# A chunked mixer trunk on one core: bank hand-overs in the planner of the order, and small copies and sums moved to ScalarE

## The chip, the core and the metric

The kernel runs on one core of a Trainium2 chip. Times are device microseconds (us) of one execution. Five engines work side by side, each through a queue of its own in order: TensorE (PE in the profile; PEld are its weight loads), VectorE (DVE), ScalarE (ACT), GpSimd (POOL) and the queue of SyncE (SP), which issues the transfers. The time before is the median of 3 runs, 2519.05 us (2516.93 to 2519.32).

## The reference

Two layers over 2048 rows of width 1024, in float32. Each layer normalises x and modulates it by a vector from c, projects it once, and gives the pieces to two groups of four heads: gated linear attention in chunks of 64 rows, and differential softmax attention. What the change touches is in the second group:

```python
q = rms_norm(q.reshape(B, S, DIFF_HEADS, 2, DIFF_DH), qn_g) * (DIFF_DH ** -0.5)
k = rms_norm(k.reshape(B, S, DIFF_HEADS, 2, DIFF_DH), kn_g)
s = einsum('bqhmd,bkhmd->bhmqk', q, k)           # two maps m a head
s = where(key_chunk <= q_chunk, s, -inf)
p = softmax(s)
o = einsum('bhqk,bkhe->bqhe', p[:, :, 0] - lam * p[:, :, 1], v)
o = rms_norm(o, g_out) * (1.0 - lam_init) * silu(z)
```

and in the first one the low-rank gate, `log_sigmoid((glr @ w_gk + b_gk)) / 16`. Both groups' outputs are projected by `w_out`, scaled by a gate and added to x.

## The kernel before

The rows are worked in units of 512 (four units a layer, `NU`), a unit in four blocks of 128 rows (`TT`). A float32 product is made of float32r ones: a matrix is split into a rounded part and the rest (`hi`, `lo`, `qh`, `ql`, `hhi`, `hlo`, `oh`, `ol`), and three of the four partial products are summed in PSUM (`mm3`). In a profile these are the acc matmuls of 128x512.

PSUM has eight banks of 512 columns. Four are the ring `acc` of the projections; the other four are one ring of tag `tp`, from which the scores (`sc`), the transposes (`tp`) and the attention outputs (`po`) are all taken.

For each unit and each of the four attention heads, `head_proj` makes a projection of 512 columns (q, k, v, z) into four acc banks. `head_evac` (line 978) takes them out: q and k to `rw`, v to `Vt`, the gate z by a tanh. `qk_gen` (line 1002) transposes q (g = 0) and k (g = 1) into one tp bank each, and forms from them the two operands of the scores. The queries need 128 partitions of which the upper and lower half hold the same: for each map m, ScalarE writes the rounded part `qh` in its own half, VectorE the rest `ql`, and both are written into the other half too (lines 1017 to 1021). `Kt` holds the rounded key in its own half and the rest in the other (lines 1023, 1024), so that one matmul with `qh` and one with `ql` give the whole score.

`attn_gen` (line 1032) takes the keys and values of earlier units back from DRAM (`Kj`, `Vj`), makes the scores of one block and map into s (128 x up to 2048), subtracting the running minimum of the negated score on VectorE, and the exponential on ScalarE with its sums `ls`. Line 1074 to 1082 form the factor `r` and the difference of both maps in `at`. `pv` (line 1085) transposes `at` in fours of 128 columns, copies them to `aT` on ScalarE, and multiplies by the values into `po`; from the sum of squares of `po` (`oss`), GpSimd makes the factor `wq`, and VectorE writes the block into `z`. `gla_gen` (line 818) makes the gate of the other group: lines 835 to 837 write the low-rank gate's rounded part, a second copy of it and its rest into `gT`, all three from the PSUM tile `gps`.

The order in which the engines get their instructions is not that of the code. `Program.record` (line 144) notes every operation with its inputs. `order` (line 244) then plays the program through with a time for each operation and each way from one engine to another, gives a tile a place in its ring when its turn comes, and always takes the operation that can start first; `best_order` (line 211) repeats that 60 times with operations moved ahead that kept TensorE waiting, and keeps the best. The instructions are issued in that order (`issue`, line 348), which is why nearly every row of the profile has line 355. When they are issued, the tile framework adds the waits. Among these is one that `order` does not know: two engines that touch one PSUM tile, reading too, take turns in the order of issue.

Of the kernel before, what the change touches and what calls it, by code (L numbers as in the profile page):

```python
# [12 lines left out]
F32 = mybir.dt.float32  # L13
# [3 lines left out]
AF = mybir.ActivationFunctionType  # L17
ALU = mybir.AluOpType
# [4 lines left out]
P = 128  # L23
# [5 lines left out]
EPS = 1e-6  # L29
# [91 lines left out]
class Program:  # L121
# [6 lines left out]

    def __init__(self, **engines):
        self.ops = []  # L130
        self.hist = {}
        self.group = {}
        self.engines = engines
# [10 lines left out]
    def record(self, e, method, args, kw):  # L144
        i = len(self.ops)
        views = [v for v in list(args) + list(kw.values()) if isinstance(v, View)]
        out = kw["out"] if "out" in kw else args[0]
        deps = set()
        for v in views:
            wr = v is out or v is kw.get("accum_out")  # L150
            h = self.hist.setdefault(v.buf, [])
            keep = []
            for j, w2, box in h:
                hit = all(a < d and c < b for (a, b), (c, d) in zip(box, v.box))
                if hit and (wr or w2) and j != i:
                    deps.add(j)
                if not (wr and all(c <= a and b <= d for (a, b), (c, d) in zip(box, v.box))):
                    keep.append((j, w2, box))
            keep.append((i, wr, v.box))
            self.hist[v.buf] = keep  # L160
        self.ops.append((e, method, args, kw, deps, self.cost(e, method, args, kw, out), {v.buf: 0 for v in views}))

    def together(self, first):

# [46 lines left out]
    def best_order(self, rounds=60):  # L211


        ops, rnd = self.ops, random.Random(0)
        turn = [float(i) for i in range(len(ops))]
        made = self.order(turn)
        best = self.span
        for _ in range(rounds):
            res, begin, end, ready = made
            lines = {e: [i for i in res if ops[i][0] == e] for e in "TAV"}  # L220
            place = {i: k for q in lines.values() for k, i in enumerate(q)}
            waits = [(begin[i] - end[j], i) for j, i in zip(lines["T"], lines["T"][1:]) if begin[i] - end[j] > 150]
            turn2 = list(turn)
            for wait, i in waits:
                if rnd.random() >= wait / 1500 * rnd.random():
                    continue
                first = begin[i] - 15000
                for _ in range(12):
                    e = ops[i][0]
                    i = max(ops[i][4], key=lambda j: end[j] + self.LAT[ops[j][0]][e], default=None)  # L230
                    if i is None or end[i] < first:
                        break
                    if (ops[i][0] in "AV" or ops[i][0] == "T" and i not in self.group) and begin[i] - ready[i] > 80:
                        q, k = lines[ops[i][0]], place[i] - 1
                        while k >= 0 and begin[q[k]] >= ready[i]:
                            turn2[i] = min(turn2[i], turn[q[k]] - 0.5)
                            k -= 1
            made2 = self.order(turn2)
            if self.span <= best:
                best, made, turn = self.span, made2, turn2  # L240
        self.span = best
        return made[0]

    def order(self, turn_of):
        ops, N = self.ops, len(self.ops)
        begin, finish = [0.0] * N, [0.0] * N
        left, uses, turn = {}, [], {}
        for o in ops:
            for b in o[6]:
# [2 lines left out]
                    turn.setdefault((b.pool, b.tag), []).append(b)  # L252
                left[b] += 1
        place = {b: k for q in turn.values() for k, b in enumerate(q)}
        nxt = dict.fromkeys(turn, 0)
        slots = {t: [{} for _ in range(q[0].bufs or q[0].pool.bufs)] for t, q in turn.items()}
        blocked = {t: [] for t in turn}
        slot, used = {}, {}
# [14 lines left out]
        while len(res) < N:  # L273
            while todo:
                now, todo = sorted(todo), []
                for i in now:
                    e, bufs = ops[i][0], ops[i][6]
                    new = {}
                    for b in sorted((b for b in bufs if b not in slot), key=place.get):
                        t = (b.pool, b.tag)  # L280
                        if place[b] != nxt[t] + new.get(t, 0) or len(slots[t]) <= new.get(t, 0):
                            blocked[t].append(i)
                            break
                        new[t] = new.get(t, 0) + 1
                    else:
                        for b in sorted(bufs, key=place.get):
                            if b not in slot:
                                t = (b.pool, b.tag)
                                slot[b] = min(slots[t], key=lambda u: max(u.values(), default=0.0))
                                slots[t].remove(slot[b])  # L290
                                used[b] = {}
                                nxt[t] += 1
                                todo += blocked[t]
                                blocked[t] = []
                            for e2, x in slot[b].items():
                                ready[i] = max(ready[i], x + (self.LAT[e2][e] if e != e2 or e == "S" else 0))
                        heapq.heappush(pend[e], (ready[i], turn_of[i], i))
# [5 lines left out]
            if rest:  # L303
                i = min(rest)[1]
                avail[e].remove(min(rest))
                heapq.heapify(avail[e])
            else:
                i = heapq.heappop(avail[e])[1]
            if e == "T":
                burst = self.group.get(i, 0)  # L310
            if e == "S":
# [31 lines left out]
                    todo += blocked[t_]  # L343
                    blocked[t_] = []
        self.span = max(free.values()) / 1e3
        return res, begin, finish, ready

    def issue(self):
        real = lambda v: v.real() if isinstance(v, View) else v
# [9 lines left out]
def trunk_kernel(ctx, tc, x, c, w_ada, b_ada, norm_g, w_in, conv_w, w_gk, b_gk, gla_norm_g,  # L359
# [458 lines left out]
    def gla_gen(l, u):  # L818
# [14 lines left out]
        gT = p_q.tile([98, 512], F32R, tag="uT", name="gT", bufs=2)  # L833
        A.activation(gT[96:98, :], ones[96:98, 0:1].to_broadcast([2, 512]), AF.Copy, scale=-1.0)
        V.tensor_copy(gT[0:32, :], gps[0:32, :])
        A.copy(gT[64:96, :], gps[0:32, :])
        V.tensor_tensor(gT[32:64, :], gps[0:32, :], gT[0:32, :].bitcast(F32), op=ALU.subtract)
        yield pe(3.5, 1.5)
        la = p_q.tile([P, TT, 256], F32, tag="q", name="la")
# [138 lines left out]
    def head_evac(l, u, hd, banks):  # L978
        key = l * NU + u
        ss = p_sm.tile([P, TT, 4], F32, tag="qss", name="qss", bufs=2)  # L980
        rq = p_sm.tile([P, TT, 4], F32, tag="rq", name="rq", bufs=2)
        sz = p_z.tile([P, TT, P], F32, tag="z", name="z")
        Vt = p_kv.tile([P, TT, P], F32, tag="V", name="Vt")
        qk = []
        for t in range(TT):
            rw = p_t.tile([P, 256], F32, tag="rw", name="rw", bufs=4)
            A.copy(rw, banks[t][:, 0:256])
            th = p_t.tile([P, P], F32, tag="th", name="th", bufs=2)
            A.activation(th, banks[t][:, 384:512], AF.Tanh, scale=0.5)
            V.scalar_tensor_tensor(sz[:, t, :], th, 1.0, banks[t][:, 384:512], op0=ALU.add, op1=ALU.mult)  # L990
            A.copy(Vt[:, t, :], banks[t][:, 256:384])
            sq = p_t.tile([P, 256], F32, tag="sq", name="sq", bufs=2)
            A.activation(sq, rw, AF.Square)
            V.tensor_reduce(ss[:, t, :], sq.rearrange("p (a n) -> p a n", a=4), axis=AX.X, op=ALU.add)
            qk.append(rw)
        rsqrt(rq.rearrange("p t a -> p (t a)"), ss.rearrange("p t a -> p (t a)"), 1.0 / 64, EPS)
        for t in range(TT):
            rv = qk[t].rearrange("p (a n) -> p a n", a=4)
            V.tensor_tensor(rv, rv, rq[:, t, :].unsqueeze(2).to_broadcast([P, 4, 64]), op=ALU.mult)
        HD[key, hd] = (qk, Vt, sz)  # L1000

    def qk_gen(l, u, hd):
# [7 lines left out]
        for g in range(2):  # L1010
# [3 lines left out]
            for m in range(2):  # L1014
                own, other = slice(64 * m, 64 * m + 64), slice(64 - 64 * m, 128 - 64 * m)
                if g == 0:
                    A.activation(qh[own, m, :], ps[own, :], AF.Copy, scale=y.G[own, :])
                    V.scalar_tensor_tensor(ql[own, m, :], ps[own, :], y.G[own, :], qh[own, m, :].bitcast(F32),
                                           op0=ALU.mult, op1=ALU.subtract)
                    A.activation(qh[other, m, :], ps[own, :], AF.Copy, scale=y.G[own, :])  # L1020
                    V.tensor_copy(ql[other, m, :], ql[own, m, :].bitcast(F32))
                else:
                    A.copy(Kt[own, m, :], ps[own, :])
                    V.tensor_tensor(Kt[other, m, :], ps[own, :], Kt[own, m, :].bitcast(F32), op=ALU.subtract)
# [7 lines left out]
    def attn_gen(l, u, hd):  # L1032
# [16 lines left out]
        def scores(qt, m):  # L1049
# [23 lines left out]
            if m == 1:  # L1073
                r = p_sm.tile([P, 2], F32, tag="r", name="r")
                V.reciprocal(r[:, 0:1], ls[:, 1:2])
                V.scalar_tensor_tensor(r[:, 0:1], r[:, 0:1], y.nlam, ls[:, 0:1], op0=ALU.mult, op1=ALU.mult)
                V.scalar_tensor_tensor(r[:, 1:2], ls[:, 0:1], EPS, ls[:, 0:1], op0=ALU.mult, op1=ALU.mult)
                at, b = q_s.pop((qt, 0)), q_s.pop((qt, 1))
                for c0 in range(0, nk, 512):
                    c1 = min(nk, c0 + 512)  # L1080
# [4 lines left out]
        def pv(qt):  # L1085
# [30 lines left out]
            junk = p_t.tile([P, P], F32, tag="th", name="junk", bufs=2)  # L1116
            ss = p_sm.tile([P, 2], F32, tag="oss", name="oss")
            A.activation(junk, o_, AF.Square, accum_out=ss[:, 0:1])
            V.scalar_tensor_tensor(ss[:, 1:2], ss[:, 0:1], 1.0 / P, r[:, 1:2], op0=ALU.mult, op1=ALU.add)
            wq = p_sm.tile([P, 1], F32, tag="wq", name="wq")  # L1120
            G.tensor_tensor(wq, ss[:, 1:2], mhalf[:, 0:1], op=ALU.pow)
            V.scalar_tensor_tensor(sz[:, qt, :], o_, wq, sz[:, qt, :], op0=ALU.mult, op1=ALU.mult)
# [205 lines left out]
```

## Time and profile before

| | |
|---|---|
| median of 3 runs | 2519.05 us |
| time of the profiled execution | 2520.62 us |
| its span, first to last instruction | 2518.9 us |
| PE busy | 2465.0 us, 98% |
| DVE busy | 1736.4 us, 69% |
| ACT busy | 1285.0 us, 51% |
| POOL busy | 136.2 us, 5% |

Shares are of the span. Busy is the time in which an engine had at least one instruction running; matmuls overlap, and their ends are modelled. 1.7 us of the execution lie outside the span.

### The profile page before, as it was taken

The numbers are of one execution on the slowest core, as the hardware profiler recorded it, in microseconds if no ns is written. First come the engines' busy times: TensorE is split into PE (matmuls) and PEld (weight loads), VectorE is DVE, ScalarE is ACT, GpSimd is POOL, SyncE is SP. The second block draws the span as 40 slices with busy tenths as digits, with TensorE's granted clock in tenths as the row PEclk, the third lists the DMA queues.
The fourth block names the chain that finished last, engine by engine and source line by source line (L and its number), as shares of the span: only waits on it lengthen the run. The fifth ranks groups of instructions, "written<-read, shape, count | busy, mean of one in ns | idle before, by whom it ended". The sixth has DMA issues, their size and how long they took to land.

```text
span 2518.9 us, 40492 instructions
## 1 busy us (share of the span) xinstructions
PE 2465.0 (98%) x13923; PEld 2025.2 (80%) x13923; DVE 1736.4 (69%) x5313; ACT 1285.0 (51%) x2760; POOL 136.2 (5%) x424
## 2 busy tenths in 40 slices
PE   8999999999999999999999999999999999999999
PEld 5787777887888888888688777888788888888887
DVE  4879767772777737677874884667636777286874
ACT  5656534562445534455763563445614556154552
POOL 0001000000000000000000010000000000000000
PEclk9999999999999999999999999999999999999999
DMA  8667876456453555444357767454474443734343
GB/s 266 251 233 281 286 247 208 156 191 211 163 186 105 189 186 172 141 136 163 109 204 267 265 247 254 169 187 153 161 251 153 142 162 119 262 102 147 130 147 126
DMA packets 204685, 474.00 MB, mean 188 GB/s; under 512 B 20736, under 2 KB 82368, under 8 KB 204480
## 3 DMA queue, kind: packets, MB, share of 16 engines
q1 hardware_dynamic: 204480, 471.41, 54.5%
q8 instruction: 111, 1.82, 0.3%
q14 instruction: 94, 0.77, 0.1%
HBM read 360.19 MB, written 111.15 MB: 187 GB/s over the span
## 4 chain that ended last, share of the span: by engine, by line
PE 79%; DVE 11%; ACT 5%; DMA 3%; issue 2%; POOL 0%; SPq 0%; POOLq 0%; ACTq 0%; DVEq 0%
PE acc L355 51%; PE sc L355 12%; PE po L355 9%; PE tp L355 7%; DVE s L355 3%; ACT qh L355 2%; DVE t L355 1%; DVE ql L355 1%; ACT s L355 1%; DMA wr<-in_w_ada_dram 1%; DVE w L355 1%; ACT t L355 1%; DVE am L355 1%; DMA Kj<-kd 1%; DVE r L355 0%
## 5 line engine op out<-in xcount | busy, mean ns | idle before, releaser
L355 PE MATMUL acc<-w,hhi 128*128 128x512 f32 x2560 | 840.5, 402 | 2.9 <-ACT w L355 1.4
L355 PEld LDWEIGHTS acc<-w,hhi 128*128 128x128 f32 x2560 | 463.7, 189 | 92.3 <-issue 4.8
L355 PE MATMUL acc<-w,hlo 128*128 128x512 f32 x1280 | 504.9, 394 | 0.0
L355 ACT ACTIVATE s<-s,mx 128x512 f32<-128x512 f32 (+15 forms) x256 | 308.2, 1204 | 291.4 <-DVE s L355 290.1
L355 PE MATMUL acc<-hhi,w 128*128 128x512 f32 x1024 | 360.0, 400 | 0.0
L355 PE MATMUL acc<-w,oh 128*128 128x512 f32 x1024 | 332.5, 398 | 2.7 <-DVE t L355 1.1
L355 DVE TENSOR_SCALAR_CACHE_REDUCE s<-sc,mx 64x64 f32<-64x64 f32 (+5 forms) x640 | 307.9, 485 | 33.0 <-PE sc L355 14.3
L355 PEld LDWEIGHTS acc<-w,hlo 128*128 128x128 f32 x1280 | 240.8, 188 | 49.0 <-issue 0.6
L355 PEld LDWEIGHTS acc<-w,oh 128*128 128x128 f32 x1024 | 189.6, 188 | 41.3 <-DVE t L355 2.6
L355 PEld LDWEIGHTS acc<-hhi,w 128*128 128x128 f32 x1024 | 192.0, 188 | 36.7 <-DVE w L355 0.4
L355 ACT COPY aT<-tp 128x512 f32<-128x512 f32 (+2 forms) x320 | 163.0, 523 | 88.2 <-PE tp L355 85.4
L355 PE MATMUL po<-Vj,aT 128*128 128x128 f32 x1536 | 204.4, 277 | 0.7 <-ACT aT L355 0.5
L355 PE MATMUL acc<-w,ol 128*128 128x512 f32 x512 | 201.5, 397 | 0.0
L355 PE MATMUL acc<-hlo,w 128*128 128x512 f32 x512 | 201.0, 393 | 0.0
L355 DVE SCALAR_TENSOR_TENSOR s<-s,r 128x512 f32<-128x512 f32 (+3 forms) x320 | 197.8, 667 | 3.0
L355 PEld LDWEIGHTS po<-Vj,aT 128*128 128x128 f32 x1536 | 190.4, 192 | 10.5 <-ACT aT L355 4.7
L355 DVE TENSOR_SCALAR_CACHE_REDUCE s<-sc 128x512 f32<-128x512 f32 (+4 forms) x256 | 158.2, 621 | 38.7 <-PE sc L355 34.5
L355 PE MATMUL tp<-ident,s 128*128 128x128 f32 x1088 | 172.9, 275 | 11.8 <-DVE ql L355 4.2
L355 PEld LDWEIGHTS tp<-ident,s 128*128 128x128 f32 x1088 | 131.9, 141 | 49.5 <-issue 12.8
L355 ACT COPY rw<-acc 128x256 f32<-128x256 f32 x128 | 48.1, 376 | 239.6 <-PE acc L355 239.6
L355 PE MATMUL sc<-Kj,qh 128*128 128x512 f32 x384 | 158.5, 413 | 3.3 <-DVE s L355 1.4
L355 ACT ACTIVATE qh<-tp,G 64x512 fp32r<-64x512 f32 x128 | 87.6, 684 | 137.1 <-PE tp L355 115.0
(183 smaller groups left out, 3682.8 us busy)
## 6 DMA issues: line engine op xcount, KB each, us to landing
w<-wd SPq DMA_DIRECT2D x424, 512.0 KB, 4.2
wd<-w SPq DMA_DIRECT2D x144, 512.0 KB, 3.7
raw<-in_w_in_dram SPq DMA_DIRECT2D x120, 256.0 KB, 5.0
Kj<-kd SPq DMA_DIRECT2D x48, 512.0 KB, 5.8
wr<-in_w_ada_dram SPq DMA_DIRECT2D x128, 128.0 KB, 3.2
kd<-Kt SPq DMA_DIRECT2D x24, 512.0 KB, 4.0
Vj<-vd SPq DMA_DIRECT2D x48, 256.0 KB, 5.4
wr<-in_w_ada_dram SPq DMA_DIRECT2D x8, 1024.0 KB, 7.4
```

The lines of the kernel that those rows point to most:

```text
L355: getattr(self.engines[e], method)(*[real(a) for a in args], **{k: real(v) for k, v in kw.items()})
```

## The change

Two things change in the planner. `order` now holds PSUM tiles apart: an operation on a PSUM tile is not begun before the last one of another engine on the same tile is over and has reached it (`bank`, `hold`), and `best_order` follows such holds back like inputs. And a ring may be passed: the second tile in line may take a place before the first, if two places are free.

Five operations change in the kernel. The second copies of `qh` and of the gate's rounded part are taken from the first copy in SBUF and not from PSUM again. The second copy of `ql` goes from VectorE to ScalarE. The copy of v stands ahead of the tanh. The square of the sum `ls` (part of `r`), and the sum that gives `oss` its second column, go from VectorE to ScalarE.

```diff
@@ order @@
-                        if place[b] != nxt[t] + new.get(t, 0) or len(slots[t]) <= new.get(t, 0):
+                        ahead = left_out[t].index(b, 0, 2) if b in left_out[t][:2] else N
+                        if len(slots[t]) <= ahead or new.get(t, 0) and ahead != new[t]:
...
+            prior = [j for b in self.banks[i] for e2, j in bank.setdefault(b, {}).items() if e2 != e]
+            if prior:
+                last = max(prior, key=lambda j: finish[j] + self.LAT[ops[j][0]][e])
+                hold = finish[last] + self.LAT[ops[last][0]][e]
+                if hold > t:
+                    held[i], ready[i] = last, hold
+                    if not rest:
+                        heapq.heappush(pend[e], (hold, turn_of[i], i))
+                        continue
+                    t = hold
+            for b in self.banks[i]:
+                bank[b][e] = i
@@ gla_gen @@
-        A.copy(gT[64:96, :], gps[0:32, :])
+        A.copy(gT[64:96, :], gT[0:32, :].bitcast(F32))
@@ head_evac @@
             A.copy(rw, banks[t][:, 0:256])
+            A.copy(Vt[:, t, :], banks[t][:, 256:384])
             th = p_t.tile([P, P], F32, tag="th", name="th", bufs=2)
             A.activation(th, banks[t][:, 384:512], AF.Tanh, scale=0.5)
             V.scalar_tensor_tensor(sz[:, t, :], th, 1.0, banks[t][:, 384:512], op0=ALU.add, op1=ALU.mult)
-            A.copy(Vt[:, t, :], banks[t][:, 256:384])
@@ qk_gen @@
-                    A.activation(qh[other, m, :], ps[own, :], AF.Copy, scale=y.G[own, :])
-                    V.tensor_copy(ql[other, m, :], ql[own, m, :].bitcast(F32))
+                    A.copy(qh[other, m, :], qh[own, m, :].bitcast(F32))
+                    A.copy(ql[other, m, :], ql[own, m, :].bitcast(F32))
@@ attn_gen, scores @@
-                V.scalar_tensor_tensor(r[:, 1:2], ls[:, 0:1], EPS, ls[:, 0:1], op0=ALU.mult, op1=ALU.mult)
+                A.activation(r[:, 1:2], ls[:, 0:1], AF.Square, scale=math.sqrt(EPS))
@@ attn_gen, pv @@
-            V.scalar_tensor_tensor(ss[:, 1:2], ss[:, 0:1], 1.0 / P, r[:, 1:2], op0=ALU.mult, op1=ALU.add)
+            A.activation(ss[:, 1:2], ss[:, 0:1], AF.Identity, scale=1.0 / P, bias=r[:, 1:2])
```

The new planner puts nearly the whole program in another order. Two places show how. The first is ScalarE's queue at the second head of the first unit, before (`qh`, `ql` and `Kt` are the score operands, `oh` a transposed output block, `w` weights, `s` scores, `oss` the sum of squares):

```order
L355 CAST w<-raw 128x512 x2
L355 ACTIVATE junk,oss<-po 128x128
L355 ACTIVATE qh<-tp,G_614 64x512 x4
L355 ACTIVATE oh<-tp,dg_619 128x512
L355 CAST Kt<-tp 64x512 x2
L355 CAST w<-raw 128x512 x4
```

and the same place after:

```order
L370 ACTIVATE oss<-oss,r 128x1
L370 CAST w<-raw 128x512 x2
L370 ACTIVATE qh<-tp,G_636 64x512 x2
L370 CAST qh<-qh 64x512 x2
L370 CAST ql<-ql 64x512 x2
L370 ACTIVATE oh<-tp,dg_643 128x512
L370 CAST Kt<-tp 64x512 x2
L370 CAST w<-raw 128x512 x2
```

Two of the four `qh` operations no longer read the tp tile, and the two `ql` copies have come into this queue, ahead of the `Kt` operations.

The second place is TensorE's queue for the same head, from the transposes of k (the second `tp<-ident,rw`) to the first score with the new key; before:

```order
L355 MATMUL tp<-ident,rw 128x128 x4
L355 MATMUL acc<-hhi,w 128x512
L355 MATMUL acc<-hlo,w 128x512
L355 MATMUL acc<-hhi,w 128x512 x2
L355 MATMUL acc<-hlo,w 128x512
L355 MATMUL acc<-hhi,w 128x512 x2
L355 MATMUL acc<-hlo,w 128x512
L355 MATMUL acc<-hhi,w 128x512 x2
L355 MATMUL acc<-hlo,w 128x512
L355 MATMUL acc<-hhi,w 128x512 x2
L355 MATMUL acc<-hlo,w 128x512
L355 MATMUL sc<-Kt,qh 128x128
```

and after, the last rows of the same stretch (in front of them stand the four transposes of k and eight more acc matmuls):

```order
L370 MATMUL acc<-hhi,w 128x512 x2
L370 MATMUL acc<-hlo,w 128x512
L370 MATMUL acc<-hhi,w 128x512 x2
L370 MATMUL acc<-hlo,w 128x512
L370 MATMUL acc<-hhi,w 128x512 x2
L370 MATMUL acc<-hlo,w 128x512
L370 MATMUL acc<-hhi,w 128x512 x2
L370 MATMUL acc<-hlo,w 128x512
L370 MATMUL acc<-hhi,w 128x512 x2
L370 MATMUL acc<-hlo,w 128x512
L370 MATMUL sc<-Kt,qh 128x128
```

Between the transposes of k and the first score stand 14 acc matmuls before and 23 after. From the transposes of q on it is 20 acc matmuls and eight transposes before, and 27 acc matmuls and eight transposes after.

## Rows read from the trace of the kernel before

**Rows 1.** The page: busy time, share of the span, instructions.
```profile
PE 2465.0 (98%) x13923; PEld 2025.2 (80%) x13923; DVE 1736.4 (69%) x5313; ACT 1285.0 (51%) x2760; POOL 136.2 (5%) x424
```

**Rows 2.** What TensorE's matmuls waited for: us in total, times, longest.
```profile
PE sc L355 <- DVE Kt L355: 7.4, 11, 1.1
...
PE tp L355 <- DVE ql L355: 4.2, 4, 1.1
PE tp L355 <- DVE s L355: 4.0, 7, 1.5
PE tp L355 <- DVE z L355: 3.1, 6, 1.5
...
PE sc L355 <- DVE s L355: 2.4, 6, 0.6
...
PE tp L355 <- ACT aT L355: 1.8, 2, 0.9
...
PE sc L355 <- DVE gT L355: 0.4, 1, 0.4
```

**Rows 3.** Timeline, second head: start, length in us; idle before, releaser in brackets.
```profile
103.14 1.38 ACT L355 ACTIVATE qh<-tp,G 64x512 fp32r<-64x512 f32 x2 [3.50 <-PE tp L355]
...
104.56 0.74 DVE L355 SCALAR_TENSOR_TENSOR ql<-tp,G,qh 64x512 fp32r<-64x512 f32 x1 [1.94 <-ACT qh L355]
...
105.33 1.38 ACT L355 ACTIVATE qh<-tp,G 64x512 fp32r<-64x512 f32 x2 [0.81 <-DVE ql L355]
105.44 0.39 PE L355 MATMUL acc<-hlo,w 128*128 128x512 f32 x1
...
105.67 0.62 PE L355 MATMUL acc<-hhi,w 128*128 128x512 f32 x2
...
107.33 1.16 ACT L355 CAST Kt<-tp 64x512 fp32r<-64x512 f32 x2
...
108.78 1.41 DVE L355 TENSOR_TENSOR Kt<-tp,Kt 64x512 fp32r<-64x512 f32 x2
...
109.51 0.33 PE L355 MATMUL sc<-Kt,qh 128*128 128x128 f32 x1 [0.94 <-DVE Kt L355]
```

**Rows 4.** Timeline at 826 us, a later head of layer 0.
```profile
826.36 1.38 ACT L355 ACTIVATE qh<-tp,G 64x512 fp32r<-64x512 f32 x2 [0.59 <-PE tp L355]
...
829.96 0.76 DVE L355 SCALAR_TENSOR_TENSOR ql<-tp,G,qh 64x512 fp32r<-64x512 f32 x1 [0.99 <-ACT qh L355]
...
830.86 0.63 PE L355 MATMUL tp<-ident,s 128*128 128x128 f32 x4 [1.05 <-DVE ql L355]
```

**Rows 5.** Timeline at 1032 us, a later head of layer 0.
```profile
1031.99 1.38 ACT L355 ACTIVATE qh<-tp,G 64x512 fp32r<-64x512 f32 x2 [0.81 <-DVE ql L355]
...
1033.40 0.59 ACT L355 COPY aT<-tp 128x512 f32<-128x512 f32 x1
...
1034.04 0.66 PE L355 MATMUL tp<-ident,s 128*128 128x128 f32 x4 [0.88 <-ACT aT L355]
```

**Rows 6.** Groups by form: operation, count, busy us, mean ns, idle before it.
```profile
L355 ACT CAST w<-raw 128x512 fp32r<-128x512 f32 x152 | 92.1, 625 | 88.1 <-PE acc L355 69.5 <-DMA wd<-w 9.6 <-DMA raw<-in_w_in_dram 4.2
...
L355 ACT ACTIVATE qh<-tp,G 64x512 fp32r<-64x512 f32 x128 | 87.6, 684 | 137.1 <-PE tp L355 115.0 <-DVE ql L355 21.2
...
L355 ACT ACTIVATE junk<-po 128x128 f32<-128x128 f32 x128 | 35.8, 280 | 121.6 <-PE po L355 120.9
...
L355 ACT ACTIVATE l<-l 128x2 f32<-128x2 f32 x2 | 0.4, 203 | 1.3 <-DVE l L355 1.3
...
L355 DVE SCALAR_TENSOR_TENSOR ql<-tp,G,qh 64x512 fp32r<-64x512 f32 x64 | 48.0, 749 | 84.0 <-ACT qh L355 80.3 <-PE po L355 3.3
...
L355 DVE CAST ql<-ql 64x512 fp32r<-64x512 f32 x64 | 27.0, 422 | 2.0
...
L355 DVE SCALAR_TENSOR_TENSOR r<-ls 128x1 f32<-128x1 f32 x128 | 19.9, 156 | 7.6 <-ACT s L355 6.2
L355 DVE SCALAR_TENSOR_TENSOR oss<-oss,r 128x1 f32<-128x1 f32 x128 | 19.7, 154 | 48.6 <-ACT junk L355 48.4
```

More of the change, by code (lines that the diff above doesn't have):

```diff
@@ L130, in __init__ @@
         self.ops = []
+        self.banks = []
         self.hist = {}
@@ L161, in record @@
         self.ops.append((e, method, args, kw, deps, self.cost(e, method, args, kw, out), {v.buf: 0 for v in views}))
+        self.banks.append({v.buf: 0 for v in views if v.buf.psum})
     def together(self, first):
@@ L218, in best_order @@
         for _ in range(rounds):
-            res, begin, end, ready = made
+            res, begin, end, ready, held = made
             lines = {e: [i for i in res if ops[i][0] == e] for e in "TAV"}
@@ L229, in best_order @@
                     e = ops[i][0]
-                    i = max(ops[i][4], key=lambda j: end[j] + self.LAT[ops[j][0]][e], default=None)
+                    i = max(ops[i][4] | {held.get(i, i)} - {i}, key=lambda j: end[j] + self.LAT[ops[j][0]][e], default=None)
                     if i is None or end[i] < first:
@@ L245, in order @@
         ops, N = self.ops, len(self.ops)
-        begin, finish = [0.0] * N, [0.0] * N
+        begin, finish, held, bank = [0.0] * N, [0.0] * N, {}, {}
         left, uses, turn = {}, [], {}
@@ L254, in order @@
         place = {b: k for q in turn.values() for k, b in enumerate(q)}
-        nxt = dict.fromkeys(turn, 0)
+        left_out = {t: list(q) for t, q in turn.items()}
         slots = {t: [{} for _ in range(q[0].bufs or q[0].pool.bufs)] for t, q in turn.items()}
@@ L291, in order @@
                                 used[b] = {}
-                                nxt[t] += 1
+                                left_out[t].remove(b)
                                 todo += blocked[t]
@@ L345, in order @@
         self.span = max(free.values()) / 1e3
-        return res, begin, finish, ready
+        return res, begin, finish, ready, held
     def issue(self):
```

## The prediction

> **What bounds the kernel now.** First the page: TensorE is busy for 98% of the span, every other engine well below [rows 1]. So the time is TensorE's own work and the places where it waits, and I read the waits next, for TensorE's matmuls alone [rows 2]. The reader is to see how small they are. The largest inside the program is that of the first score with a new key for VectorE's part of it (`Kt`), 7.4 us at 11 places; the next, 4.2 us at 4 places, is a transpose that wants a PSUM tile which `ql` is still reading. The matmuls themselves are the same before and after, so nothing but these waits, and others like them, can be gained or lost: all that the rows name comes to a few tens of us, about 1% of the time.
>
> Then I went to the places on the timeline. At the second head the transposes of q are done and ScalarE starts the first two `qh` at 103.14 [rows 3]. Both read the q tile. VectorE's `ql`, which reads it too, starts at 104.56, when both are over. The next two `qh` start at 105.33, when `ql` is over, having idled 0.81 us with the releaser `ql`, though they need nothing from it: it is the turn on the tile that they wait for. Only behind the fourth `qh` come the `Kt` operations at 107.33, and VectorE's `Kt` at 108.78. TensorE had run out of what stood ahead of the first score and sat idle for 0.94 us up to 109.51. The same ping-pong ends otherwise at 826 us [rows 4]: the tile is held from 826.36 to 829.96 + 0.76 = 830.72, that is 4.36 us, and a transpose that takes its place in the ring idles 1.05 us, until 830.86. At 1032 us [rows 5] it is an `aT` copy that stands on ScalarE behind the second pair of `qh`, and a transpose loses 0.88 us. The planner of before counted on none of this, as it let ScalarE and VectorE read a tile at one time; the order that it wrote has too little TensorE work in front of these three kinds of place.
>
> An idle microsecond in these rows is a little more in lost time. A matmul of 512 columns is shown 0.39 us long, but the next starts 0.23 us after it (105.44 to 105.67) [rows 3]; the 0.16 us of overlap are lost too when the next one waits. Lost time is thus the idle time plus 0.16 us a wait.
>
> **The change part by part.** *The key.* In the new order ScalarE does at this head: two `qh` from the tile (2 x 0.684), two copies of them in SBUF, two copies of `ql`, one `oh`, two `Kt` (1.16). No row shows ScalarE copying 64x512 from SBUF; the nearest are the 128x512 cast from SBUF, 0.625, and from above the 64x512 from PSUM with a factor, 0.684 [rows 6]; below, half of the 1.16 of the two `Kt`, 0.58 [rows 3]. I take 0.625, the same source and the same rounding. The first `Kt` part of VectorE is then ready 1.37 + 1.25 + 1.25 + 0.69 (`oh`, priced as `qh`) + 1.16 + 0.70 (half of 1.41) = 6.4 us after the first `qh`, against 108.78 + 0.70 - 103.14 = 6.3 us before. So the chain to the key is not shorter. What changes is TensorE's side. Before, it came to the first score at 109.51 - 0.94 - 0.16 = 108.41, that is 5.3 us after the first `qh`, with 20 matmuls of 512 columns and 8 transposes since the transposes of q. Now 27 and 8 stand there: 7 x 0.23 = 1.6 us more, 6.9 us, which covers the 6.4 with 0.5 to spare. At all 32 heads, counted with 0.23 us for a matmul of 512 columns and a transpose as half of one, this stretch was shorter than 5.5 us 12 times; after, 4 times, and in those four the order puts the first `Kt` ahead of at least one of the two `ql` copies, which takes 0.6 us or more out of the chain. So I let all 11 waits go: 7.4 + 11 x 0.16 = 9.2 us. If the four copies cost 0.684 each, the chain is 0.24 us longer and still covered.
>
> *The tile of q.* It is read by two `qh` and then two `ql`: 2 x 0.684 + 2 x 0.749 = 2.9 us, where it was held 4.36 us. The 1.46 us saved are more than the 1.05 us that the transpose waited, and the order leaves as much in front of that transpose as before (ten matmuls of 512 columns, where nine stood, beside the same others). 4.2 + 4 x 0.16 = 4.8 us go. What is late next there is the transpose's own data, s, which this trace shows ready.
>
> *aT behind the ping-pong.* ScalarE no longer waits 0.81 us for `ql` between two pairs of `qh` [rows 5], so the copy comes that much sooner, nearly all of the 0.88 us: 2 x (0.81 + 0.16) = 1.9 us, if the new copies stand behind it.
>
> *The gate's copy.* The copy to `gT` from SBUF takes ScalarE's turn out of the tile; TensorE waited for it 0.4 us once [rows 2], and that goes.
>
> *v ahead of the tanh.* VectorE's z stood behind all three of ScalarE's reads of the bank before, and does now: nothing, unless z stood between tanh and v before.
>
> *Work moved.* VectorE loses the 64 `ql` copies (27.0 us), the 128 squares (19.9) and the 128 sums (19.7) [rows 6]: 66.6 us, and comes to 1670. ScalarE gains 64 x 0.625 = 40, loses 64 x 0.059 = 4 on the `qh` copies, and gains 256 operations on one column. Nearest for those is the exponential of two columns, 0.203; above it 128 columns with a sum, 0.280 [rows 6]. With 0.203 it is 52 us, in all +88, and 1373 us, 55% of the span; with 0.280 +108. None of it lies on TensorE's path by itself; ScalarE's share of the span leaves room, and the sum `oss` now follows its squares on the engine that made them. From this I take nothing. For the range I keep 6 us lost (a dozen new waits of 0.35 + 0.16 us behind ScalarE's new operations) and 6 us gained (half of the waits for VectorE's s and z, 4.0 + 3.1 + 2.4 us at 19 places, with their overlap [rows 2]).
>
> A rule of the Trainium skill speaks against this part. "ScalarE: Activation LUTs", section "Rules for kernel authors", gives copies, sums and products to VectorE and keeps ScalarE for functions. By this trace the rule prices it rightly: 66.6 us of VectorE become 88 to 108 us of ScalarE; engine time that nobody waits for is not in the sum, though. Were it to count, it would do so by way of ScalarE's queue: the slower rival below.
>
> The sum: 9.2 + 4.8 + 1.9 + 0.4 = 16.3 us less. The profiled execution took 2520.6 us (span 2518.9 and 1.7 around it), so it would be 2504.3; the median of the three runs lies 1.6 below that execution, which gives 2519.05 - 16.3 = 2502.7.
>
> **Rivals.** *ScalarE becomes late (slower).* Four copies now stand on ScalarE between the last `qh` and `Kt` at most heads, and what comes behind them waits 2.5 us. The point from which it decides is the 0.5 us to spare at the head above. If a copy takes 0.9 us and not 0.625 (nothing in the rows shows one from SBUF to the other half of the partitions), the four are 1.1 us longer and the key 0.6 late; at 20 heads that is 20 x (0.6 + 0.16) = 15 us where 9.2 were lost before. An `aT` copy behind them would cost TensorE the same 0.6 + 0.16 at some ten heads, 7.6 us, and the 1.9 us of the term on `aT` would not come. With 4.8 + 0.4 still saved: 15 - 9.2 + 7.6 - 5.2 = 8 us more, 2527. For it: the chain is no shorter than before, and the rule just named prices such copies as a loss. Against: all forms of 512 columns on ScalarE in [rows 6] lie between 0.58 and 0.69 us, whatever they read.
>
> *The waits move (no change).* The search for the order starts anew, and the places it cured may come back elsewhere: transposes for s, z for the output, the boundary between the layers. If 13 of the 16.3 us come back as new waits, the time is 2515.8. For it: the rest of the waits in [rows 2] are of kinds that the change does not touch, and the order is new everywhere. Against: the new planner sees the turns on the tiles, so what it leaves is less by surprise.
>
> *VectorE was the tighter engine (much faster).* 66.6 us off VectorE also take the waits for s and z away, 9.5 us and 19 x 0.16 = 3 us. Then it is 2502.7 - 12.5 = 2490. For it: VectorE is at 69%, the busiest after TensorE. Against: at such places ScalarE is in the same chain.
>
> **How the numbers follow.** Forecast (2494 to 2511): 0.70. VectorE's relief: 0.12. Waits move: 0.11. ScalarE late: 0.07. The likeliest case gives 2502.7. The range 2489 to 2516 leaves out the slower case, and part of the two others. About 0.2%, 5 us, is what can be told from no change here; faster than 2514 is the forecast, the relief and a small part of the third: 0.84; within: 0.09; slower: 0.07.
>
> **What would show it.** In the waits of TensorE: `Kt` under 1.5 us (now 7.4), `ql` under 1 us (now 4.2), both as idle time. On ScalarE's timeline no wait between the first two `qh` and the rest, and the q tile held about 3 us. VectorE near 1670 us, ScalarE 1360 to 1400. TensorE's matmul work unchanged. I am wrong if the time falls without these two waits going, or if they go and the time stays: then others have come, and the waits name them; wrong in the step on ScalarE if `aT` or `Kt` of ScalarE rise in that list above 5 us.

## The result, and the profile after

The changed kernel takes 2493.85 us (median of 4 runs, 2492.93 to 2495.07) against 2519.19 us (4 runs, 2516.93 to 2520.24) for the kernel before on the same chip: a ratio of 0.9894, with a 95% interval of 0.9880 to 0.9908. The medians differ by 25.3 us (their own ratio would be 0.9899). The forecast was 2502.7 us, 16.3 less: the direction and the range of 2489 to 2516 held, and the gain was 9 us larger than its sum. The time lies just under the band that the forecast gave its own case (2494 to 2511), and nearer to the 2490 of the rival on VectorE's relief than to 2502.7. The profiled execution took 2492.93 us, with a span of 2491.1.

The engines' line of the page after, busy time, share of the span and instructions, to be laid beside [rows 1]:

```profile
PE 2454.7 (99%) x13923; PEld 2027.2 (81%) x13923; DVE 1690.3 (68%) x4993; ACT 1369.9 (55%) x3080; POOL 133.0 (5%) x424
```

TensorE still sets the time. VectorE fell by 46 us, not by 67, to 1690; ScalarE came to 1370, inside the 1360 to 1400 of the forecast. What TensorE's matmuls waited for after (us in total, times, longest):

```profile
PE tp L370 <- DVE s L370: 6.2, 8, 2.2
PE tp L370 <- DMA wr<-in_w_ada_dram: 4.8, 2, 3.9
PE tp L370 <- DMA crow<-in_c_dram: 2.5, 1, 2.5
PE po L370 <- ACT aT L370: 2.4, 3, 2.0
PE sc L370 <- DVE am L370: 2.2, 3, 1.3
PE tp L370 <- DVE z L370: 1.9, 2, 1.6
...
PE sc L370 <- DVE s L370: 1.7, 3, 0.9
```

The reader is to see what is missing against [rows 2], also from the rows left out here: no row for `Kt`, none for `ql`, none for a transpose that waits for `aT`, none for `gT`. But the two rows for s together have risen, from 4.0 + 2.4 to 6.2 + 1.7 us: not every wait fell. Over all rows of the two lists, TensorE's idle time fell from 47.4 us at 69 places to 30.5 at 36.

The second head of the first unit, in the timeline after (start, length; idle before and releaser in brackets), beside [rows 3]:

```profile
102.62 1.39 ACT L370 ACTIVATE qh<-tp,G 64x512 fp32r<-64x512 f32 x2
...
104.04 1.26 ACT L370 CAST qh<-qh 64x512 fp32r<-64x512 f32 x2
104.05 1.53 DVE L370 SCALAR_TENSOR_TENSOR ql<-tp,G,qh 64x512 fp32r<-64x512 f32 x2 [0.60 <-ACT qh L370]
...
105.32 1.26 ACT L370 CAST ql<-ql 64x512 fp32r<-64x512 f32 x2
...
106.61 0.69 ACT L370 ACTIVATE oh<-tp,dg 128x512 fp32r<-128x512 f32 x1
...
107.19 1.16 ACT L370 CAST Kt<-tp 64x512 fp32r<-64x512 f32 x2
...
108.39 1.41 DVE L370 TENSOR_TENSOR Kt<-tp,Kt 64x512 fp32r<-64x512 f32 x2 [0.30 <-ACT Kt L370]
...
109.38 0.22 PE L370 MATMUL sc<-Kt,qh 128*128 128x128 f32 x1
```

The tile of q is held from 102.62 to 104.05 + 1.53 = 105.58, that is 2.96 us (forecast 2.9). Half of the key is ready at 108.39 + 0.70 = 109.09, 6.5 us after the first `qh` (forecast 6.4); TensorE comes at 109.38, 6.8 us after it (forecast 6.9), and its score matmul has no bracket: it didn't wait. The forms whose prices had to be guessed, after (operation, count, busy us, mean ns, idle before):

```profile
L370 ACT CAST qh<-qh 64x512 fp32r<-64x512 f32 x64 | 39.6, 619 | 1.4
L370 ACT CAST ql<-ql 64x512 fp32r<-64x512 f32 x64 | 39.6, 619 | 1.5 <-DVE ql L370 0.2
L370 ACT ACTIVATE oss<-oss,r 128x1 f32<-128x1 f32 x128 | 37.9, 296 | 3.2
...
L370 ACT ACTIVATE r<-ls 128x1 f32<-128x1 f32 x128 | 25.5, 199 | 1.6
```

A copy from SBUF costs 619 ns (taken: 625). The square of one column costs 199 (taken: 203), but the sum with its factor and its added column 296, above the upper bound of 280 taken from [rows 6].

So every step read at this head came true in the trace. That does not show that it was the cause of the 25 us. For that, the parts of the change were taken apart.

### The profile page after: what moved, and what is told of

It reads as the page before. It is cut to its first block, busy times and chain, and to the rows that moved or that the text cites. A ratio compares the mean times of both kernels' runs of the same rounds, so it can differ in the third digit from the quotient of the medians.

```text
span 2491.1 us, 40404 instructions
## 1 busy us (share of the span) xinstructions
PE 2454.7 (99%) x13923; PEld 2027.2 (81%) x13923; DVE 1690.3 (68%) x4993; ACT 1369.9 (55%) x3080; POOL 133.0 (5%) x424
## 4 chain that ended last, share of the span: by engine, by line
PE 83%; DVE 8%; DMA 4%; ACT 2%; issue 2%; POOL 0%; SPq 0%; POOLq 0%; DVEq 0%; ACTq 0%
PE acc L370 54%; PE sc L370 11%; PE po L370 10%; PE tp L370 8%; DVE s L370 3%; DMA wr<-in_w_ada_dram 2%; DVE t L370 1%; DMA wd<-w 1%; DVE am L370 1%; DVE w L370 1%; DMA xt<-in_x_dram 1%; ACT s L370 1%; DMA raw<-in_w_in_dram 0%; ACT qh L370 0%; SPq L370 0%
## 5 line engine op out<-in xcount | busy, mean ns | idle before, releaser
L370 DVE SCALAR_TENSOR_TENSOR s<-s,r 128x512 f32<-128x512 f32 (+2 forms) x320 | 197.8, 667 | 2.7
L370 ACT CAST w<-raw 128x512 fp32r<-128x512 f32 x152 | 93.5, 627 | 107.4 <-PE acc L370 89.5
```

What stands on the lines that cost most here:

```text
L370: getattr(self.engines[e], method)(*[real(a) for a in args], **{k: real(v) for k, v in kw.items()})
```

## The experiments

Two measures are used. The first is the ratio to the kernel before, from runs on the same chip; the row "after" is the result above, the others come from three later sessions of five rounds each. A ratio of two medians differs from the one given by up to 0.09%. The second is TensorE's lost time, worked out from each profiled execution: the start of each matmul less the start of the one before, less the median of that step for the same three shapes in a row. What is taken off this way sums to between 2380 and 2386 us in every kernel here, so what differs by more than that lies in the lost time. It counts idle time and overlap together, and it is that of one execution. With the medians taken over all fourteen kernels, the rows come out 1 to 3 us lower. I split the lost time by what released the matmul: the four kinds of place of the forecast (`Kt`, `ql`, a transpose behind `aT`, `gT`), and all others. Of the others, some 52 to 65 us in every kernel are small excesses for which the profile names no releaser. "Edits" are the five places changed in the kernel's own code, six operations in all.

| kernel | holds | passing | edits | ratio (95%) | lost us | four kinds | others |
|---|---|---|---|---|---|---|---|
| before | no | no | no | 1 | 124.6 | 18.7 | 105.9 |
| before, other seed | no | no | no | 1.0018 (1.0009 to 1.0027) | 130.1 | 19.1 | 111.0 |
| edits alone | no | no | all | 0.9988 (0.9979 to 0.9997) | 122.5 | 7.2 | 115.3 |
| passing alone | no | yes | no | 0.9994 (0.9985 to 1.0003) | 125.5 | 15.7 | 109.8 |
| holds alone | yes | no | no | 0.9962 (0.9950 to 0.9975) | 117.1 | 2.8 | 114.3 |
| holds, edits | yes | no | all | 0.9985 (0.9976 to 0.9994) | 123.2 | 5.3 | 117.9 |
| same, other seed | yes | no | all | 0.9948 (0.9931 to 0.9965) | 113.0 | 2.5 | 110.5 |
| holds, passing | yes | yes | no | 0.9909 (0.9893 to 0.9924) | 103.3 | 1.5 | 101.8 |
| same, other seed | yes | yes | no | 0.9940 (0.9927 to 0.9952) | 103.9 | 0.2 | 103.7 |
| holds, passing, query | yes | yes | query | 0.9895 (0.9876 to 0.9914) | 97.0 | 0.1 | 96.9 |
| SBUF rings only | yes | SBUF | all | 0.9907 (0.9892 to 0.9922) | 102.1 | 1.2 | 100.9 |
| after | yes | yes | all | 0.9894 (0.9880 to 0.9908) | 97.7 | 0.2 | 97.5 |
| after, other seed | yes | yes | all | 0.9901 (0.9886 to 0.9916) | 102.2 | 0.4 | 101.8 |
| third in line too | yes | 3 deep | all | 0.9899 (0.9885 to 0.9912) | 102.3 | 0.9 | 101.4 |

**The planner's two parts without the edits.** All five edits are undone:

```diff
-                    A.copy(qh[other, m, :], qh[own, m, :].bitcast(F32))
-                    A.copy(ql[other, m, :], ql[own, m, :].bitcast(F32))
+                    A.activation(qh[other, m, :], ps[own, :], AF.Copy, scale=y.G[own, :])
+                    V.tensor_copy(ql[other, m, :], ql[own, m, :].bitcast(F32))
...
```

> The planner's parts of the change alone (held-apart PSUM tiles, passed rings); the five edits of the kernel's own instructions are undone. Theory 1 (the two parts share the gain: a planner that knows the bank holds puts more matmuls ahead of the key steps, the copies from SBUF free the query tile early): TensorE's wait for Kt falls from 7.4 us to under 2, its wait for ql stays at 3 to 5 us since the query tile is still read four times (held over 4 us), and the time is about 2508 us (2504 to 2513). Rival A (the edits do it all, the planner only reshuffles): 2515 to 2523, Kt above 5 us. Rival B (the planner does it all): 2492 to 2498, ql under 1 us.

It took 2499.46 us against 2521.74: 22 us of the gain are there without a single edit. In its list of TensorE's waits `Kt` has no row. Of the four kinds the list keeps 0.3 us at `gT` and the first of these two rows; the second is a score that waits for `ql` as its operand, not a transpose that waits for the tile:

```profile
PE tp L370 <- ACT aT L370: 0.7, 1, 0.7
PE sc L370 <- DVE ql L370: 0.7, 1, 0.7
```

So the wait for the tile is gone, though nothing frees the tile of q sooner (at the second head `ql` ends 4.34 us after the first `qh` starts): my theory, that the copies from SBUF free it in time, is wrong in this. The time lies between rival B's range and my theory's, nearer to rival B.

**The edits alone**, with the planner of before:

> The five edits of instructions alone, with the planner of before. Theory 1: the query tile is held about 3 us, ql falls from 4.2 to under 1 us, Kt stays at 5 us or above because the old planner still counts on the bank's two readers running side by side; about 2512 us (2508 to 2517). Rival A (edits do it all): 2492 to 2498. Rival B (planner does it all): 2516 to 2522. If taking 66 us of work from VectorE were what pays, this run would also lie near 2500, with falls in waits that have nothing to do with query and key.

It took 2518.69 us, in rival B's range. From its page and its list of TensorE's waits:

```profile
PE 2465.6 (98%) x13923; PEld 2026.5 (81%) x13923; DVE 1690.5 (67%) x4993; ACT 1363.9 (54%) x3080; POOL 136.2 (5%) x424
...
PE sc L355 <- DVE Kt L355: 1.7, 4, 0.7
PE tp L355 <- DVE ql L355: 1.7, 6, 0.3
```

`Kt` and `ql` lost much of their size (1.7 us idle each; my theory had `Kt` at 5 or more and `ql` under 1), and the time came back elsewhere: the four kinds lose 11.5 us, the others gain 9.4. VectorE's busy time was 1690.5 us, as low as after, and the time fell by 0.12%. The rival that VectorE's relief pays by itself is out.

**The planner and the query copies.** The three smaller edits are undone:

```diff
-        A.copy(gT[64:96, :], gT[0:32, :].bitcast(F32))
+        A.copy(gT[64:96, :], gps[0:32, :])
-                A.activation(r[:, 1:2], ls[:, 0:1], AF.Square, scale=math.sqrt(EPS))
+                V.scalar_tensor_tensor(r[:, 1:2], ls[:, 0:1], EPS, ls[:, 0:1], op0=ALU.mult, op1=ALU.mult)
...
```

> The planner's parts plus the two query copies from SBUF; the gate copy, the place of the copy of V and the row sums' squares are as before. Theory 1: Kt and ql both under 1.5 us, the time 2495 to 2502 us. Rival C (the relief of VectorE by the squares, 28 us of its work, gives a good part of the rest): 2503 to 2509, with VectorE at about 1718 us busy.

It took 2494.57 us, the time of the whole change and 0.4 us under my theory's range, with VectorE at 1711.6 us:

```profile
PE 2456.3 (99%) x13923; PEld 2029.5 (81%) x13923; DVE 1711.6 (69%) x5249; ACT 1324.6 (53%) x2824; POOL 134.5 (5%) x424
```

The gate's copy, the place of the copy of v and the 256 small operations together are worth nothing that can be told.

**No passing.** The changed kernel, with the old rule on the line:

```diff
-                        if len(slots[t]) <= ahead or new.get(t, 0) and ahead != new[t]:
+                        if ahead != new.get(t, 0) or len(slots[t]) <= ahead:
```

> The changed kernel, but a ring's second tile may not be given out ahead of its first (the rule of before). Theory 1: the passing adds little, since the query and key waits rest on holds and copies: 2492 to 2498 us. Rival D (passed rings give a good part): 2500 us or above, with waits on ring buffers (w, aT, Kt) that the changed kernel lacks.

It took 2518.76 us: in this order nearly all of the gain was gone. I had expected the passing to add little, and of my expectations this one missed by the most. These waits of TensorE rose (in the changed kernel `po` behind `aT` had 2.4 us, and the two others no row):

```profile
PE po L370 <- ACT aT L370: 6.9, 10, 1.7
...
PE sc L370 <- DMA Kj<-kd: 3.7, 5, 1.1
PE sc L370 <- DVE Kt L370: 3.5, 2, 2.3
```

`Kj` are the keys of earlier units, loaded by DMA. One of the two places of `Kt` shows that a row's name is not a mechanism. Its place in the timeline of this kernel:

```profile
1436.33 0.58 ACT L370 CAST Kt<-tp 64x512 fp32r<-64x512 f32 x1
...
1439.48 0.49 DVE L370 SCALAR_TENSOR_TENSOR am<-wr,cact,am 128x256 f32<-128x256 f32 x1 [2.67 <-DMA wr<-in_w_ada_dram]
1440.00 0.69 DVE L370 TENSOR_TENSOR Kt<-tp,Kt 64x512 fp32r<-64x512 f32 x1
...
1440.84 0.45 PE L370 MATMUL sc<-Kt,qh 128*128 128x128 f32 x1 [2.27 <-DVE Kt L370]
```

ScalarE's part of the key is over at 1436.91. VectorE's part starts only at 1440.00, since it is queued behind `am`, which waited 2.67 us for a weight's DMA. No turn on a tile is in it; a row `Kt` in the list would have been put down to the ping-pong.

**Passing alone, and which rings.** In the first kernel the holds are taken out of the planner (and the edits undone); in the second only SBUF rings may be passed:

```diff
-            prior = [j for b in self.banks[i] for e2, j in bank.setdefault(b, {}).items() if e2 != e]
+            prior = []
...
-                        if len(slots[t]) <= ahead or new.get(t, 0) and ahead != new[t]:
+                        if len(slots[t]) <= ahead or (new.get(t, 0) or b.psum) and ahead != new.get(t, 0):
```

> The kernel before with one thing changed: the second tile in a ring's line may be placed ahead of the first. No holds on PSUM tiles, none of the five edits. After the runs without passing (2516 to 2519 us, whether or not Kt and ql had gone) the theory of the forecast has fallen as to what carries the time. Theory P (passing gives TensorE other work wherever a ring's line was stuck, and that is nearly all of the gain): 2498 to 2504 us, with some of Kt and ql left in TensorE's waits (3 us or more together), since the planner still knows nothing of the turns on a tile. Theory H (holds and passing are needed together; either alone gives nothing): 2514 us or above.

> The changed kernel, but only SBUF rings may be passed (keys K, queries and their like q, transposed probabilities and scratch t2, th, mx and so on); the ring of PSUM tiles keeps its order. Theory S (what gets stuck is the line for SBUF buffers: an operation that reads a PSUM tile can't begin for lack of a place for its output): 2492 to 2497 us, as the changed kernel. Theory T (the line for PSUM tiles is what matters, since TensorE's groups wait for a tile): 2510 us or above.

Passing alone took 2519.25 against 2519.99 us: nothing, which is theory H. The two largest waits of the forecast are still in its list:

```profile
PE sc L368 <- DVE Kt L368: 7.0, 9, 1.2
...
PE tp L368 <- DVE ql L368: 2.5, 4, 1.0
```

With the holds but passing only SBUF rings it was 2497.80, most of the gain: theory S, if 0.8 us above its range. The line for PSUM tiles matters by no more than two seeds differ.

**The search's luck.** The order comes from a randomized search, so four of the kernels were run from another seed as well:

```diff
-        ops, rnd = self.ops, random.Random(0)
+        ops, rnd = self.ops, random.Random(1)
```

> The changed kernel with another random seed in the search for the order. If the gain belongs to the change: 2491 to 2499 us. If it was a lucky search: above 2505 us.

> The changed kernel without passing (as the run before), and the search for the order started from another random seed. It tells how far the search's luck moves the time. If passing is what counts: 2512 to 2520 us. If the run without passing was an unlucky search: under 2505 us.

> The kernel before with another random seed in the search for the order. It tells whether the 2519 us from which the gain is counted was a poor draw. If the gain of 25 us belongs to the change: 2512 to 2524 us, with Kt and ql again the largest waits inside the program. If a good part of it is the draw: under 2508 us.

The change itself gave 2496.00 us, so it was not a lucky draw. Before gave 2526.51 against 2521.25, 2.5 us above its expected range, so 2519 was not a poor draw. Without passing it was 2507.43, between the two answers that were expected, where the first seed had taken 2518.76: here luck moves the time by 0.37%, and the first seed makes passing look larger than the other does. Both orders without passing lie above every kernel with holds and passing in the lost time (113.0 and 123.2 against 97.0 to 103.9).

> Holds and passing without the five edits, with another random seed. With seed 0 it took 2499.5 us, and the changed kernel took 2493.9 and 2496.0 with two seeds. If the edits are worth some 4 us beyond the scatter: 2497 to 2503 us. If the planner alone does all and the rest is scatter: 2493 to 2496 us.

This took 2508.33 us, above all that was expected. Its five executions spread from 2501.92 to 2509.41, and the profiled one was the fastest, 6.4 us under the median, so that its lost time (103.9) flatters it. By the ratio it can't be told from the second run without passing, which has the edits (0.9940 and 0.9948). The edits are worth 0.15% by one seed (0.9909 to 0.9894) and 0.39% by the other (0.9940 to 0.9901). As two seeds of one kernel differ by 0.07 to 0.37%, a gain is likely, but these runs don't settle its size.

**The holds alone.**

> The kernel before with the holds on PSUM tiles in its planner alone: no passing of rings, none of the five edits. Passing alone gave nothing (2519.3), holds and passing without the edits 2499.5, holds and edits without passing 2518.8 and 2507.4 from two seeds. Theory H (holds and passing pay only together): Kt and ql leave TensorE's waits (under 2 us each in the kind of place the forecast described), other waits come in their stead (s, z, aT, w), and the time is 2508 to 2522 us. Rival (the holds carry the gain and the two runs without passing were poor orders): 2499 to 2505 us.

It took 2512.16 us, inside theory H's range, yet 0.38% less than before: the holds alone do give something. Its list of TensorE's waits (us in total, times, longest):

```profile
PE tp L370 <- DVE s L370: 4.8, 8, 1.5
PE tp L370 <- DVE oss L370: 3.1, 3, 1.5
PE po L370 <- ACT aT L370: 2.9, 5, 0.7
PE sc L370 <- DVE s L370: 2.6, 5, 0.8
...
PE tp L370 <- DVE vN L370: 1.9, 2, 1.6
PE acc L370 <- ACT w L370: 1.8, 2, 1.0
...
PE sc L370 <- DMA Kj<-kd: 1.3, 5, 0.4
...
PE sc L370 <- DVE Kt L370: 0.3, 1, 0.3
```

`Kt` is down from 7.4 to 0.3 us and `ql` has no row. At the second head (timeline):

```profile
102.80 2.77 ACT L370 ACTIVATE qh<-tp,G 64x512 fp32r<-64x512 f32 x4 [3.51 <-PE tp L370]
...
105.60 1.53 DVE L370 SCALAR_TENSOR_TENSOR ql<-tp,G,qh 64x512 fp32r<-64x512 f32 x2 [3.78 <-ACT qh L370]
...
108.86 1.41 DVE L370 TENSOR_TENSOR Kt<-tp,Kt 64x512 fp32r<-64x512 f32 x2
109.88 0.22 PE L370 MATMUL sc<-Kt,qh 128*128 128x128 f32 x1
```

The tile of q is held from 102.80 to 107.13, 4.33 us, as long as the 4.36 of [rows 4]. Still nothing waits: the four `qh` stand in one run, and TensorE is given enough to come to the key 7.1 us after the first of them, where it came after 5.3 in [rows 3]. But of the 15.9 us that the four kinds lose, only 7.5 stay: `oss`, `vN` and the weights' copies have come.

Are the two parts needed together? With the edits, passing on top of the holds is worth 0.91 and 0.47% by the two seeds, both above 0.37%, the most by which two seeds of one kernel differ. Without the edits it is 0.53% by the first seed, but only 0.22% if the second order with holds and passing (0.9940) is taken. Holds alone give 0.38% and passing alone 0.06%, one seed each; both together give 0.91% by one seed and 0.60% by the other. The first is about twice the sum, the second is above it by less than seeds move the time. So that passing needs the holds to pay, and the holds passing to pay in full, is shown by one seed.

**What passing does that can be seen.** The loads of earlier units' keys, in the view of that tile, for the holds alone (durations in ns as least, median, greatest; then the first and the last start in us):

```profile
L370 PE MATMUL sc<-Kj,qh x384: 387/393/504, 344.9 to 2462.3; 128*128 128x512 f32 x192
...
L370 SPq DMA_DIRECT2D Kj<-kd x48: 319/424/1572, 338.7 to 2404.2; - x48
...
DMA to landing us min/median/max: 4.3/6.3/8.7
```

and for holds with passing, both without the edits:

```profile
L370 PE MATMUL sc<-Kj,qh x384: 387/390/504, 340.8 to 2448.5; 128*128 128x512 f32 x192
...
L370 SPq DMA_DIRECT2D Kj<-kd x48: 319/424/1094, 302.1 to 2390.4; - x48
```

The first load is issued 6 us ahead of the matmul that reads it without passing, and 39 us ahead with it. Over all 48, the shortest lead is 4.3 us and 16 are under 8 us in the one; in the other none is under 23.7. A load lands 4.3 to 8.7 us after its issue, so without passing TensorE comes to old keys, at those 16, about when they land, and it waited for them 5 times. In lost time the keys' loads are 2.4 us of the 13.8 between these two kernels (117.1 to 103.3); transposes behind `oss` are 3.6, projections behind the weights' copies 3.4, transposes behind `vN` 2.2, s 2.2; other kinds, up to about 2 us each, rise and fall and cancel. Passing alone gave the loads the same lead (none under 23.7) and saved nothing, so a lead by itself is not the gain.

**The third in line.** A version that might beat both:

```diff
-                        ahead = left_out[t].index(b, 0, 2) if b in left_out[t][:2] else N
+                        ahead = left_out[t].index(b, 0, 3) if b in left_out[t][:3] else N
```

> The changed kernel, but the third tile in a ring's line may be placed too, if enough places are free (the first two stay behind it in line). If a stuck line still costs TensorE work after the change: 2485 to 2492 us. If passing one tile already frees what can be freed: 2492 to 2498 us, within the scatter of the seeds.

It took 2496.00 us, a ratio of 0.9899, within what seeds move. The changed kernel keeps the lowest median of all, by less than seeds move.

## Why the prediction was right or wrong, point by point

- **What bounds the kernel**: right. The matmuls' own steps sum to 2380 to 2386 us in every kernel; the rest of the differences is lost time.
- **The key** (9.2 us): right in the trace (9.8 to 0.2 in lost time), and the reading of the cause, that the planner of before let two engines read one tile at one time, is borne out: the holds alone take it to 1.0, with no edit. The edits alone leave 1.7 of 7.4 us idle, so the holds do not have this term to themselves.
- **The tile of q** (4.8): gone, in full, but the stated cause failed. The forecast gave it to the shorter hold, 2.9 us for 4.36. With the tile held 4.33 us it is gone as well. No transpose waits there any more in the order that the holds give; the copies need not have been made for it. With the copies alone (edits, old planner) 1.7 us at 6 places stay, so a shorter hold by itself didn't clear it either.
- **aT behind the ping-pong** (1.9) and **the gate's copy** (0.4): 2.4 and 1.7 in lost time, both gone. ScalarE's wait for `ql` between its `qh` operations is gone as forecast (21.2 us in [rows 6], 1.4 us before the new `qh` copies in the rows above), but a transpose behind `aT` has no row with the holds alone either. The gate's term was under-sized: the list shows one place, lost time five, short ones that the list leaves out. The four terms together: 16.3 forecast, 18.7 - 0.2 = 18.5 measured.
- **The step that failed** is what the sum left out: that the passed rings have no term, and that all other waits stay as they are. The others went from 105.9 to 97.5, 8.4 us (by the other seed from 111.0 to 101.8, 9.2 us), which is nearly the whole 9 us by which the forecast fell short; the two profiled executions differ by 27.7 us, of which the four terms are 18.5. The path there is not one of small changes: the holds alone raise them to 114.3, passing takes them down to 101.8, the edits to 97.5 (seed 0 throughout; the last step is no larger than two seeds differ).
- **Where luck helped**: the time fell into the range, but 7.1 of the 16.3 us (the tile, `aT`, the gate) were credited to the copies, and most of that goes without them; and a term that was not in the sum brought about as much as the sum had too little.
- **Rival "the waits move"** (0.11): it did not come true for the change, but for the holds alone it is half true. Of 15.9 us 8.4 came back. The edits alone show it more plainly: 9.4 of 11.5 came back. The argument against it, that a planner that sees the turns leaves less by surprise, does not hold without passing.
- **Rival "VectorE was the tighter engine"** (0.12): its time, 2490, was nearest of the rivals' and nearer than the forecast's, and for the wrong reason. With VectorE at 1690 us the edits alone gained 0.12%, and leaving 21 us of small operations on VectorE (1711.6, planner and query copies) cost nothing that can be told.
- **Rival "ScalarE becomes late"** (0.07): out. The copy costs 619 ns and not 900, `Kt` has no row, `aT` 2.4 us. (The argument against it held, though the bounds of 0.58 to 0.69 us are not those of all such forms: the trace before has one of 512 columns at 0.72 us.) "ScalarE: Activation LUTs" of the Trainium skill, section "Rules for kernel authors", gives additions and products to VectorE; copies, which the prediction added, aren't in it. That ScalarE is the dearer engine for them is borne out (the square 199 ns for 156, the sum 296 for 154; in all ScalarE gained 85 us for 46 of VectorE), but it did not lengthen the time of this kernel.
- **VectorE near 1670**: missed by 20 us. The three groups that were moved, 66.6 us by their mean durations, are gone, and the durations of all its operations sum to 64 us less (1998 to 1934). But its busy time fell by 46: the sum of 1998 stands against 1736 busy, so operations overlap their neighbours, and their durations overstate what the engine gets back. The short ones do most: the 256 operations on one column, 39.6 us by duration, gave back 21 us (1711.6 to 1690.3), the `ql` copies 25 of 27. I had taken durations for busy time. No term hung on it. ScalarE's 1370 against a forecast of 1373 is partly luck: its durations grew by 98 us, not 88, and its busy time by 85.

What stays open: which SBUF ring carries the gain of passing and by what it gains, since earlier loads alone do not pay; what the edits give under the new planner (0.15 to 0.39%) place by place; and, as neither part was run alone from a second seed, nor passing with the edits but without holds, how far the two parts need each other.

## What to carry to other kernels

A planner that learns a true constraint can lose much of what it gains (here 8.4 of 15.9 us) while another rule that it keeps, here that buffers are given out in one fixed order, stands in its way: test the parts singly and together. When a wait is taken out of a program that is searched anew, count what returns, over all the other waits, before crediting it. And run another seed of any randomized order before reading a cause into less than half a per cent.

## What was not expected of the hardware

An operation of one column on ScalarE is not one price: the square took 199 ns, the sum with a factor and an added column 296. The Trainium skill, "ScalarE: Activation LUTs", section "What ACT_TABLE_LOAD costs", states that each operand given as a pointer to a column adds about 93 ns to an ACTIVATE; the 97 ns between the two rows agree, though the two rows differ in their function too.
